# The scan's output kept channel-major: the state as the stationary operand, the decay as a loaded tile, the skip term through DRAM

## The chip, the cores and the metric

The kernel runs on one core of a Trainium2 chip. The metric is device time in microseconds (us) of one execution; lower is better. One further execution was recorded by the hardware profiler, and all rows shown here come from it.

## What is computed

Two layers of a diffusion backbone run over 128 context tokens and 512 latent tokens: layer 0 is gated attention, layer 1 a bidirectional state-space scan (Mamba-2 SSD). The change is in layer 1's scan. Cut to what matters:

```python
def ssd_chunked(x, a, b, c, h0):           # chunks of 128 tokens, 4 groups of 8 heads of 64 channels
    a_cs = jnp.cumsum(a, axis=2)
    decay = jnp.exp(jnp.where(lower, a_cs[:, :, :, None] - a_cs[:, :, None, :], -jnp.inf))
    cb = jnp.einsum('bclgn,bcsgn->bclsg', c, b)
    y_diag = jnp.einsum('bclsgr,bcsgrp->bclgrp', cb[..., None] * decay, x)
    states = jnp.einsum('bclgn,bclgrp->bcgrpn', b, x * decay_end[..., None])
    ...                                     # h_prev: the state ahead of each chunk
    y_off = jnp.einsum('bclgn,bcgrpn->bclgrp', c, h_prev) * jnp.exp(a_cs)[..., None]
    return (y_diag + y_off).reshape(Bs, T, H, P), h_final
...
    y = y_f + flip(y_b) + d_skip.astype(f32)[:, None] * xs
    y = rms_norm(y.reshape(B, T, D_INNER) * jax.nn.silu(z), gnorm_w)
    return y @ w_out, h_f, h_b
```

## The kernel before

The 640 tokens are five tiles `t` of 128 (t=0 is the context, t=1 to 4 the latents). Layer 1 (`layer1`, L1010) first projects; then four groups `g` of 8 heads run one after the other, and within a group a loop over ten steps `j` (L1240) lays out the scan, in the midst of which the projections for the next group (`x_unit`, `bc_unit`) and for the gate (`z_unit`) are placed. A projection is 48 matmuls (L914) into one of two PSUM buffers `pj`; `conv_chunk` then takes it through three DVE steps, a tanh on ACT and a last DVE step (L994 to L999) into a tile `u` (two buffers) or `B0`/`B1`. `x_turn` transposes `u` on PE so that tokens lie on partitions, and ACT copies that into `xt`. Weights come in through SP's DMA queue and are split in two parts by ACT (L73) and by DVE or POOL (L74).

The scan of a group, in the program's order:

- `y_init` (L1107): POOL writes the skip term, `xt` times the head's skip weight, into Y, tokens on partitions.
- `a_load`, `decay`: the logarithms of the decay come by DMA from DRAM (`acd`), broadcast over partitions, into tiles `am0` (two buffers) and `am1` (one buffer); POOL masks them (L1116, L1117), ACT takes 16 exponentials (L1121), POOL adds the two directions (L1122). `mix` multiplies by C times B (PE L1127, DVE L1128).
- `off` (L1173 to L1175), twice per step for the two directions: PE multiplies C (stationary) with the state `H` (512 columns); DVE multiplies the result in PSUM by exp of the cumulated decay, a column `ea` broadcast over each head's 64 channels, and adds it to Y.
- `diag` (L1135 to L1140): 16 half-width matmul instructions give the chunk's own part with channels on partitions; four transposes on PE (L1138) turn Y round; ACT copies the diagonal part into Y (L1139), and DVE adds the turned Y (L1140). From here on Y is channel-major.
- `advance` (L1179 to L1183) moves the state on; `weighted` (POOL) and `prompt_state` (L1151) belong to the states.
- `gate` multiplies Y by the gate and stores it to DRAM (`yzd`, L1091); in group 3 `gate_last` does so tile by tile, and the output projection (L1368) begins within the group.

The order of the instructions on each engine is laid out by the framework's scheduler, which goes by a model of the engines and by which instruction is ready; each engine, and SP's DMA queue, then works in that order. Two PSUM pools exist: `pj` (two buffers of two banks) and `a` (four of one bank), the latter for all small results.

Of the kernel before, what the change touches and what calls it, by code (L numbers as in the profile page):

```python
# [10 lines left out]
AF = mybir.ActivationFunctionType  # L11
ALU = mybir.AluOpType
# [4 lines left out]
P = 128  # L17
D = 1024
KD = D // P
NT = 5  # L20
# [5 lines left out]
SH = 32  # L26
NG = 4
# [8 lines left out]
def uoff(t):  # L36
    return col0(t) - 1
# [16 lines left out]
class Hybrid:  # L54
# [862 lines left out]
    def dt_stage(self, hT, wp, pj, pa, sp, wk):  # L917
        nc, A = self.nc, self.A
        w = self.load_w(wp, A["l1_w_in"], [(DI + DI + 2 * NG * P, 64)])
        W = NT * 64  # L920
# [3 lines left out]
        ones, al, db = misc[:, 0:P], misc[:, P:P + 64], misc[0:64, 199:200]  # L924
        packs = [self.tl(wk, [P, 3, NT, 64], tag=t_, bufs=b_) for t_, b_ in (("am0", 2), ("am0", 2), ("am1", 1))]
        slots = iter([p_[:, i] for p_ in packs for i in range(3)])
        self.dsk = self.tl(sp, [P, SH], tag="dsk")
        for d, s in enumerate(("f", "b")):
            nc.sync.dma_start(out=db[32 * d:32 * d + 32, :], in_=A[f"l1_dt_bias_{s}"].unsqueeze(1))
            nc.sync.dma_start(out=al[:, 32 * d:32 * d + 32], in_=A[f"l1_a_log_{s}"].unsqueeze(0).to_broadcast([P, 32]))  # L930
        nc.sync.dma_start(out=self.dsk, in_=A["l1_d_skip"].unsqueeze(0).to_broadcast([P, SH]))
        nc.scalar.activation(al, al, AF.Exp)
        ps = self.proj_T(pj, w, 0, 64, hT)
        dtv = self.tl(wk, [64, TW], tag="Wl", bufs=1)
# [6 lines left out]
        T = lambda nme, pool=None: next(slots) if pool is None else self.tl(pool, shp, tag=nme)  # L941
        v, u, s, s2, p_, dt = T("sv"), T("su"), T("ss_"), T("ss2"), T("spp"), T("sdt")
# [21 lines left out]
        acs = T("sacs")  # L964
# [1 line left out]
        nc.vector.memset(ones, 1.0)  # L966
        ptot = self.tl(pa, shp, tag="a")
        nc.tensor.matmul(ptot, ones, a_, start=True, stop=True)
        self.ea, self.cd, self.ws, self.nb = T("ea", sp), T("cd", sp), T("ws", sp), T("nb", sp)
        nc.scalar.activation(self.ea, acs, AF.Exp)  # L970
        nc.scalar.activation(self.cd, ptot, AF.Exp)
        nc.vector.tensor_tensor(self.ws, ptot, acs, op=ALU.subtract)
        nc.scalar.activation(self.ws, self.ws, AF.Exp)
# [3 lines left out]
        pr = self.tl(pj, [P, 1024], tag="pj")  # L977
        for t in range(NT):
            nc.tensor.transpose(pr[0:64, P * t:P * t + P], acs[:, t, :], self.ident)
        at = self.tl(wk, [64, NT * P], tag="Wh", bufs=1)  # L980
        nc.scalar.copy(at, pr[0:64, 0:NT * P])
        self.acd = [[self.tl(self.dp, [2, 8, P], tag=f"acd{t}{g}") for g in range(NG)] for t in range(NT)]
        for g in range(NG):
            for d in range(2):
                for t in range(NT):
                    r0 = 32 * d + 8 * g
                    nc.sync.dma_start(out=self.acd[t][g][d], in_=at[r0:r0 + 8, P * t:P * t + P])

    def conv_chunk(self, j, w, off, hT, pj, u):
        nc = self.nc  # L990
# [19 lines left out]
    def layer1(self, hT, wp, pj, pa, ctx):  # L1010
        nc, tc, A, O = self.nc, self.tc, self.A, self.O
        sp = self.pool("s1", ctx=ctx)
        self.weng = [nc.gpsimd]
        wk = self.pool("s2", bufs=2, ctx=ctx)
        self.fss = self.tl(self.cp, [P, NT], tag="fss")
        self.one = self.tl(self.cp, [P, 1], tag="one")
        nc.vector.memset(self.one, 1.0)
        self.ssq = self.tl(sp, [P, NT, P], tag="ssq")
        self.yzd = [self.tl(self.dp, [P, NT, 4, P], tag=f"yzd{g}") for g in range(NG - 1)]
        Y = self.Y = self.tl(sp, [P, NT, 4, P], tag="ys")  # L1020
        bcs, xts, zss, W, Xw, H, St = {}, {}, {}, {}, {}, {}, {}
        wcur = {}

        def x_unit(g, jj):
# [4 lines left out]
            wcur["u"] = self.conv_chunk(4 * g + jj, wcur["x"], P * (jj % 2), hT, pj, self.tl(wk, [P, TW - 3], tag="u"))  # L1029

        def x_turn(g, jj):
            xt = xts[g]
            self.turn(wcur["u"], pa, lambda t, ps: nc.scalar.copy(xt[:, t, P * jj:P * jj + P], ps))

        def bc_unit(g, which):
            if which == 0:
# [63 lines left out]
        bch = lambda ap: ap.unsqueeze(2).to_broadcast([P, 8, HD])  # L1100
        h3 = lambda ap: ap.rearrange("p (h d) -> p h d", d=HD)
        sl = lambda g, d: slice(32 * d + 8 * g, 32 * d + 8 * g + 8)
        ts = lambda t: slice(uoff(t), uoff(t) + P)

        def y_init(g, t):
            y = Y[:, t].rearrange("p j q -> p (j q)")
            nc.gpsimd.tensor_tensor(h3(y), h3(xts[g][:, t, :]), bch(self.dsk[:, 8 * g:8 * g + 8]), op=ALU.mult)  # L1107

        def a_load(g, t):
            af = W[g, t] = [self.tl(wk, [P, 8, P], tag=f"am{d}", bufs=2 - d) for d in range(2)]  # L1110
            for d in range(2):
                nc.sync.dma_start(out=af[d].rearrange("p h l -> p (h l)"), in_=self.acd[t][g][d].rearrange("h l -> (h l)").unsqueeze(0).to_broadcast([P, 8 * P]))
# [17 lines left out]
        def diag(g, t):  # L1130
            w = W.pop((g, t))[0]
            pd = self.tl(pa, [P, 4, P], tag="a")
            for h in range(8):
                e = 64 * (h % 2)
                nc.tensor.matmul(pd[e:e + 64, h // 2, :], xts[g][:, t, HD * h:HD * h + HD], w[:, h, :], start=True, stop=True)  # L1135
            pr = self.tl(pa, [P, 4, P], tag="a")
            for i in range(4):
                nc.tensor.transpose(pr[:, i, :], Y[:, t, i, :], self.ident)  # L1138
            nc.scalar.copy(Y[:, t], pd)  # L1139
            nc.vector.tensor_tensor(Y[:, t], Y[:, t], pr, op=ALU.add)  # L1140

        def weighted(g, t, d):
            xw = Xw[g, t, d] = self.tl(wk, [P, 512], tag=f"xw{d}", bufs=2)
# [24 lines left out]
            nc.scalar.copy(H[d], ps.rearrange("p j q -> p (j q)"))  # L1168

        def off(g, t, d):  # L1170
            y = Y[:, t].rearrange("p j q -> p (j q)")
            ps = self.tl(pa, [P, 512], tag="a")
            nc.tensor.matmul(ps, bcs[g][1][:, ts(t)], H[d], start=True, stop=True)  # L1173
            nc.vector.tensor_tensor(h3(ps), h3(ps), bch(self.ea[:, t, sl(g, d)]), op=ALU.mult)
            nc.vector.tensor_tensor(y, y, ps, op=ALU.add)  # L1175

        def advance(g, t, d):
            p2 = self.tl(pa, [P, 512], tag="a")
# [49 lines left out]
        for g in range(NG):  # L1228
# [11 lines left out]
            for j in range(10):  # L1240
# [19 lines left out]
                    diag(g, t)  # L1260
                if j < 4:
                    a_load(g, seq[j + 1])
                if j <= 2:
                    for d in range(2):
                        weighted(g, j + 1 if d == 0 else 4 - j, d)
# [199 lines left out]
```

## Time and profile before

| | |
|---|---|
| time, three runs | 996.47 us median (991.88 to 997.28) |
| profiled execution | 996.55 us, of which 994.8 us are the span from the first to the last instruction |
| busy share of the span | PE 94%, DVE 66%, ACT 52%, POOL 43% |
| mean granted clock of PE | 0.981 of full speed |
| DMA | 127.91 MB, on average 129 GB/s |

PE is TensorE's matmul, PEld its weight loads, DVE VectorE, ACT ScalarE, POOL GpSimd, SP SyncE (which only issues DMAs here). Busy shares are averages over stages with different limits. "a <- b" in a list of waits reads: a waited, and b ended the wait; an engine's name with a "q" is its sequencer. L12 is line 12 of the kernel.

### The profile page before, as it was taken

The page shows a single profiled execution, that of the slowest core. Times are in us where ns is not written, and L with a number is a line of the kernel's source. Part 1 is how long each engine was busy: PE and PEld are TensorE (multiplying, and loading weights), DVE is VectorE, ACT ScalarE, POOL GpSimd, SP SyncE. Part 2 cuts the span into 40 slices and gives each one's busy share as a digit, 9 for nine tenths or more (in the row PEclk, how much of TensorE's full clock was granted, in tenths as well). Part 3 has the DMA queues.
Part 4 walks back from the last instruction along what each step waited for, and adds up shares of the span by engine and source line. Part 5 has one row for each costly group of instructions (what it writes and reads, how often), then busy time and mean ns, then how long its engine had stood idle before and what let it go on. Part 6 is the DMA issues. An engine that isn't in the chain of part 4 may idle for free. (4 is left out here: it accounts for less than half of the span.)

```text
span 994.8 us, 17000 instructions
## 1 busy us (share of the span) xinstructions
PE 937.9 (94%) x6466; PEld 835.0 (84%) x6466; DVE 656.3 (66%) x1046; ACT 515.3 (52%) x1212; POOL 431.1 (43%) x415
## 2 busy tenths in 40 slices
PE   5998999999999989989899979999999999989998
PEld 3897879879997789989898878889988898658786
DVE  5468665666675764884759854956587547797663
ACT  5355666757775763433446564446436642554240
POOL 3345235227270162364267475739484853333000
PEclk9999999999999989999999999999999999989999
DMA  9942234221113222333234352344524441455752
GB/s 319 351 128 87 86 127 138 67 73 43 37 49 107 85 93 100 123 106 89 86 131 148 121 181 88 109 139 145 151 87 146 156 133 64 128 183 190 257 194 96
DMA packets 90354, 127.91 MB, mean 129 GB/s; under 512 B 6816, under 2 KB 65312, under 8 KB 90272
## 3 DMA queue, kind: packets, MB, share of 16 engines
q1 hardware_dynamic: 90272, 126.82, 39.6%
q8 instruction: 51, 0.84, 0.3%
q14 instruction: 31, 0.25, 0.1%
HBM read 115.10 MB, written 11.70 MB: 127 GB/s over the span
## 5 line engine op out<-in xcount | busy, mean ns | idle before, releaser
L914 PE MATMUL pj<-h,wh 128*128 128x322 f32 (+1 forms) x1248 | 298.3, 325 | 8.7 <-DVE B L999 7.5
L914 PEld LDWEIGHTS pj<-h,wh 128*128 128x128 f32 (+1 forms) x1248 | 211.2, 189 | 21.5 <-issue 14.0
L74 POOL TENSOR_TENSOR wl<-raw,wh 128x512 fp32r<-128x512 f32 (+1 forms) x70 | 133.1, 1912 | 184.6 <-ACT wh L73 182.9
L914 PE MATMUL pj<-h,wl 128*128 128x322 f32 (+1 forms) x624 | 198.6, 319 | 0.0
L73 ACT CAST wh<-raw 128x1024 fp32r<-128x1024 f32 (+1 forms) x117 | 103.0, 912 | 79.7 <-DMA raw<-in_l_w_out 22.4
L1121 ACT ACTIVATE am<-am,nb 128x128 f32<-128x128 f32 x320 | 97.9, 389 | 62.4 <-POOL am L1117 39.9
L914 PEld LDWEIGHTS pj<-h,wl 128*128 128x128 f32 (+1 forms) x624 | 118.2, 190 | 3.9 <-issue 3.6
L283 PE MATMUL pp<-wh,big 128*128 128x256 f32 x576 | 112.1, 284 | 0.5 <-ACT sg L527 0.5
L283 PEld LDWEIGHTS pp<-wh,big 128*128 128x128 f32 x576 | 91.2, 188 | 0.9 <-ACT sg L527 0.7
L74 DVE TENSOR_TENSOR wl<-raw,wh 128x1024 fp32r<-128x1024 f32 x47 | 62.8, 1347 | 38.0 <-ACT wh L73 38.0
L283 PE MATMUL pp<-wl,big 128*128 128x256 f32 x288 | 81.1, 282 | 0.0
L74 DVE TENSOR_TENSOR pl<-pt,ph 128x512 fp32r<-128x512 f32 (+1 forms) x100 | 59.2, 599 | 25.9 <-ACT ph L73 25.1
L633 DVE TENSOR_REDUCE nm<-S 128x1 f32<-128x640 f32 x64 | 52.3, 819 | 13.7 <-PE S L630 12.7
L73 ACT CAST ph<-pt 128x512 fp32r<-128x512 f32 (+1 forms) x100 | 51.4, 517 | 19.1 <-PE pt L658 14.3
L1122 POOL TENSOR_TENSOR am<-am,am 128x1024 f32<-128x1024 f32 x20 | 48.7, 2437 | 26.2 <-ACT am L1121 26.2
L637 ACT ACTIVATE Pt<-S,nm 128x640 f32<-128x640 f32 x64 | 51.2, 802 | 13.4 <-PE pt L658 9.9
L1368 PE MATMUL pj<-wh,h 128*128 128x512 f32 x160 | 54.4, 413 | 0.5 <-ACT wh L73 0.5
L283 PEld LDWEIGHTS pp<-wl,big 128*128 128x128 f32 x288 | 54.3, 188 | 0.0
L658 PE MATMUL pt<-cst,Pt 128*128 128x128 f32 x320 | 51.6, 279 | 2.6 <-DVE pl L74 2.3
L630 PE MATMUL S<-kT,qT 128*128 128x320 f32 x256 | 51.1, 324 | 2.3 <-ACT Pt L637 2.3
L1116 POOL TENSOR_SCALAR_AFFINE_SELECT am<-am 128x1024 f32<-128x1024 f32 x20 | 24.2, 1211 | 56.6 <-DMA am<-acd 32.3
L658 PEld LDWEIGHTS pt<-cst,Pt 128*128 128x128 f32 x320 | 37.2, 142 | 11.8 <-PE S L630 3.7
(347 smaller groups left out, 2135.9 us busy)
## 6 DMA issues: line engine op xcount, KB each, us to landing
raw<-in_l_w_in SPq DMA_DIRECT2D x48, 512.0 KB
am<-acd SPq DMA_DIRECT2D x40, 512.0 KB
raw<-in_l_w_out SPq DMA_DIRECT2D x36, 512.0 KB
og<-in_l_mod_w SPq DMA_DIRECT2D x29, 512.0 KB
raw<-in_l_w_in SPq DMA_DIRECT2D x25, 256.0 KB
mw<-in_l_mod_w SPq DMA_DIRECT2D x11, 512.0 KB
raw<-in_l_mod_w SPq DMA_DIRECT2D x8, 512.0 KB
yzd<-ys SPq DMA_DIRECT2D x6, 640.0 KB
```

The lines of the kernel that those rows point to most:

```text
L73: (heng.tensor_copy if heng else self.nc.scalar.copy)(hi, src)
L74: (eng or self.nc.vector).tensor_tensor(lo, src, r32(hi), op=ALU.subtract)
L283: nc.tensor.matmul(ps, a[:, k, cs], b[:, k, :], start=k == 0 and a is hi and b is w[0], stop=k == KD - 1 and a is lo)
L630: nc.tensor.matmul(S[:, 192 + 320 * q:512 + 320 * q], qTs[g, t][:, h, :], kT[:, hl, 320 * q:320 * q + 320], start=hl == 0, stop=hl == 1)
L633: nc.vector.tensor_reduce(c["m"], c["s"], axis=AX.X, op=ALU.max, negate=True)
L637: nc.scalar.activation(Pt, c["s"], AF.Exp, bias=c["m"], scale=1.0, accum_out=rss[g][t][:, h:h + 1])
L658: nc.tensor.transpose(pt[:, 2 * i + j, :], Pts[j][:, kt * P:kt * P + P], self.ident)
L914: nc.tensor.matmul(ps[0:m, 190 + 322 * half:512 + 322 * half], w[b][:, k, off:off + m], hT[s][:, k, 322 * half:322 * half + 322], start=fi ...
L1116: nc.gpsimd.affine_select(out=af[0], in_=af[0], pattern=[[0, 8], [1, P]], base=0, channel_multiplier=-1, compare_op=ALU.is_ge, fill=NEG)
L1121: nc.scalar.activation(af[d][:, h, :], af[d][:, h, :], AF.Exp, bias=self.nb[:, t, i:i + 1], scale=1.0)
L1122: nc.gpsimd.tensor_tensor(af[0], af[0], af[1], op=ALU.add)
L1368: nc.tensor.matmul(self.PS[t][n], y[a][:, kk, :], b, start=k0 + k == 0 and i == 0, stop=k0 + k == 15 and i == 2)
```

## The change

Y stays channel-major from the start. In `off` the state becomes the stationary operand (four matmuls of 128 columns) and C the moving one. The factor exp(cumulated decay) now varies along the free axis and differs by partition half, so it is computed once for all (`et`), stored to DRAM (`ecd`) and loaded, broadcast over 64 partitions twice, into a tile E (four buffers) by a new function `e_load`. The skip term is made by ACT from `u`, in place and after `u` has been transposed, stored to DRAM (`dud`), and loaded into Y by `y_init`. `diag` adds its PSUM result to Y with one DVE operation; the four transposes and ACT's copy go, and with them the tile `ea`.

```diff
-        self.dsk = self.tl(sp, [P, SH], tag="dsk")
+        self.dsk = self.tl(sp, [P, SH // 2], tag="dsk")
...
-        nc.sync.dma_start(out=self.dsk, in_=A["l1_d_skip"].unsqueeze(0).to_broadcast([P, SH]))
+        dv = A["l1_d_skip"].rearrange("(c a) -> a c", a=2)
+        for a in range(2):
+            nc.sync.dma_start(out=self.dsk[64 * a:64 * a + 64, :], in_=dv[a].unsqueeze(0).to_broadcast([64, SH // 2]))
...
-        nc.scalar.activation(self.ea, acs, AF.Exp)
...
+        et = self.tl(wk, [64, NT * P], tag="Wl", bufs=1)
+        nc.scalar.activation(et, at, AF.Exp)
+        self.ecd = self.tl(self.dp, [64, NT * P], tag="ecd")
+        nc.sync.dma_start(out=self.ecd, in_=et)
...
         def x_turn(g, jj):
-            xt = xts[g]
-            self.turn(wcur["u"], pa, lambda t, ps: nc.scalar.copy(xt[:, t, P * jj:P * jj + P], ps))
+            xt, u = xts[g], wcur["u"]
+            self.turn(u, pa, lambda t, ps: nc.scalar.copy(xt[:, t, P * jj:P * jj + P], ps))
+            nc.scalar.activation(u, u, AF.Copy, scale=self.dsk[:, 4 * g + jj:4 * g + jj + 1])
+            nc.sync.dma_start(out=self.dud[g][:, 1:5, jj, :], in_=u[:, 0:4 * P].rearrange("p (t q) -> p t q", q=P))
+            nc.sync.dma_start(out=self.dud[g][:, 0, jj, :], in_=u[:, uoff(0):uoff(0) + P])
...
         def y_init(g, t):
-            y = Y[:, t].rearrange("p j q -> p (j q)")
-            nc.gpsimd.tensor_tensor(h3(y), h3(xts[g][:, t, :]), bch(self.dsk[:, 8 * g:8 * g + 8]), op=ALU.mult)
+            nc.sync.dma_start(out=Y[:, t], in_=self.dud[g][:, t])
...
-            pr = self.tl(pa, [P, 4, P], tag="a")
-            for i in range(4):
-                nc.tensor.transpose(pr[:, i, :], Y[:, t, i, :], self.ident)
-            nc.scalar.copy(Y[:, t], pd)
-            nc.vector.tensor_tensor(Y[:, t], Y[:, t], pr, op=ALU.add)
+            nc.vector.tensor_tensor(Y[:, t], Y[:, t], pd, op=ALU.add)
+
+        def e_load(g, t, d):
+            e = E[d] = self.tl(wk, [P, 4, P], tag="E", bufs=4)
+            r = 32 * d + 8 * g
+            for a in range(2):
+                src = self.ecd[r:r + 8, P * t:P * t + P].rearrange("(j a) l -> a j l", a=2)[a]
+                nc.sync.dma_start(out=e[64 * a:64 * a + 64], in_=src.unsqueeze(0).to_broadcast([64, 4, P]))
...
         def off(g, t, d):
-            y = Y[:, t].rearrange("p j q -> p (j q)")
-            ps = self.tl(pa, [P, 512], tag="a")
-            nc.tensor.matmul(ps, bcs[g][1][:, ts(t)], H[d], start=True, stop=True)
-            nc.vector.tensor_tensor(h3(ps), h3(ps), bch(self.ea[:, t, sl(g, d)]), op=ALU.mult)
-            nc.vector.tensor_tensor(y, y, ps, op=ALU.add)
+            ps = self.tl(pa, [P, 4, P], tag="a")
+            for j in range(4):
+                nc.tensor.matmul(ps[:, j, :], H[d][:, P * j:P * j + P], bcs[g][1][:, ts(t)], start=True, stop=True)
+            nc.vector.tensor_tensor(ps, ps, E[d], op=ALU.mult)
+            nc.vector.tensor_tensor(Y[:, t], Y[:, t], ps, op=ALU.add)
...
                 if j < 4:
                     a_load(g, seq[j + 1])
+                    for d in range(2):
+                        e_load(g, j + 1 if d == 0 else 4 - j, d)
```

## Rows read from the trace of the kernel before

**Rows 1.** The page: busy time, share of the span, instructions.

```profile
PE 937.9 (94%) x6466; PEld 835.0 (84%) x6466; DVE 656.3 (66%) x1046; ACT 515.3 (52%) x1212; POOL 431.1 (43%) x415
```

**Rows 2.** Busy time by stretch: length, engines (instructions), PE clock, DMA share, GB/s.

```profile
500.00:850.00 350.00, 337.89 (x2248) 304.86 (x2247) 229.30 (x272) 178.62 (x447) 214.60 (x149) 1.00 0.41 129
850.00:915.00 65.00, 58.06 (x286) 43.92 (x285) 55.63 (x69) 35.90 (x69) 21.47 (x26) 0.92 0.54 173
915.00:995.00 80.00, 74.92 (x323) 60.02 (x321) 45.03 (x57) 21.79 (x25) 1.59 (x1) 1.00 0.52 179
```

**Rows 3.** What PE waited for from 500 to 850 us: total, times, longest.

```profile
PE pj L914 <- DVE B L999: 7.5, 2, 5.2
PE a L1138 <- DVE ys L1175: 1.8, 3, 1.0
```

**Rows 4.** The same list of waits, 850 to 915 us.

```profile
PE a L1135 <- DVE ys L1175: 2.3, 1, 2.3
PE a L1138 <- DVE ys L1175: 1.8, 1, 1.8
```

**Rows 5.** L1138 alone by stretch: PE and PEld busy (instructions), clock, DMA.

```profile
500.00:850.00 350.00, 10.33 (x64) 6.95 (x64) 1.00 0.41 129
850.00:915.00 65.00, 2.54 (x16) 1.75 (x16) 0.92 0.54 173
```

**Rows 6.** Chain of waits: start us, us, what, how many.

```profile
802.83 7.18 PE pj L914 x48
810.01 0.87 PE a L1166 x8
```

**Rows 7.** Timeline of PE: start us, us, line, operation, tiles, shapes, how many.

```profile
569.03 1.02 PE L1173 MATMUL a<-h,B 128*128 128x512 f32 x2
569.88 1.05 PE L1151 MATMUL a<-T,xw 128*128 128x128 f32 x8
```

**Rows 8.** Line L1151, its weight loads: ns least/median/most, first and last start.

```profile
L1151 PEld LDWEIGHTS a<-T,xw x64: 186/192/192, 569.5 to 896.1; 128*128 128x128 f32 x64
```

**Rows 9.** Groups, 440 to 850 us: busy us, mean ns | idle before, releasers.

```profile
L1175 DVE TENSOR_TENSOR ys<-ys,a 128x512 f32<-128x512 f32 x28 | 18.9, 680 | 4.8 <-POOL ys L1107 4.3
...
L1107 POOL TENSOR_TENSOR ys<-xt,dsk 128x512 f32<-128x512 f32 x20 | 21.1, 1088 | 12.9 <-DMA yzd<-ys 4.6 <-ACT xt L1033 4.4 <-DVE xt L1058 2.1
...
L998 ACT ACTIVATE pj<-u 128x641 f32<-128x641 f32 x16 | 11.2, 701 | 33.1 <-DVE u L996 33.1
...
L1140 DVE TENSOR_TENSOR ys<-ys,a 128x512 f32<-128x512 f32 x16 | 10.9, 683 | 18.2 <-ACT ys L1139 18.1
...
L1139 ACT COPY ys<-a 128x512 f32<-128x512 f32 x16 | 9.3, 579 | 27.5 <-PE a L1138 18.8 <-issue 8.8
```

**Rows 10.** Loads of the state, their issue on SP: ns least/median/most.

```profile
L1160 SPq DMA_DIRECT2D st<-in_state_bwd_l x4: 453/478/516, 446.6 to 701.9; - x4
```

**Rows 11.** The page: the DMA queue's packets, MB, share of 16 engines.

```profile
q1 hardware_dynamic: 90272, 126.82, 39.6%
```

**Rows 12.** Chain of waits, near the end: two landings, a store's and a load's.

```profile
925.68 3.96 DMA out_y_sample<-ym
...
937.50 2.64 DMA u<-yzd
```

**Rows 13.** Timeline of ACT, SP and DVE around the reuse of a buffer `u`.

```profile
644.81 0.24 ACT L1033 COPY xt<-a 128x128 f32<-128x128 f32 x1
...
637.51 15.62 SPq L1112 DMA_DIRECT2D am<-acd  x3
...
655.00 0.95 DVE L994 TENSOR_SCALAR u<-pj,cw,cols 128x641 f32<-128x641 f32 x1 [0.34 <-PE pj L914]
```

**Rows 14.** Timeline of ACT and DVE in group 0; brackets: idle time, releaser.

```profile
574.68 2.45 ACT L1121 ACTIVATE am<-am,nb 128x128 f32<-128x128 f32 x8 [3.12 <-POOL am L1117]
...
577.63 0.69 DVE L1140 TENSOR_TENSOR ys<-ys,a 128x512 f32<-128x512 f32 x1 [4.63 <-ACT ys L1139]
...
579.71 1.22 DVE L1128 TENSOR_TENSOR am<-am,a 128x1024 f32<-128x1024 f32 x1 [1.39 <-POOL am L1122]
```

More of the change, by code (lines that the diff above doesn't have):

```diff
@@ L968, in dt_stage @@
         nc.tensor.matmul(ptot, ones, a_, start=True, stop=True)
-        self.ea, self.cd, self.ws, self.nb = T("ea", sp), T("cd", sp), T("ws", sp), T("nb", sp)
-        nc.scalar.activation(self.ea, acs, AF.Exp)
+        self.cd, self.ws, self.nb = T("cd", sp), T("ws", sp), T("nb", sp)
         nc.scalar.activation(self.cd, ptot, AF.Exp)
@@ L1018, in layer1 @@
         self.ssq = self.tl(sp, [P, NT, P], tag="ssq")
+        self.dud = [self.tl(self.dp, [P, NT, 4, P], tag=f"dud{g}") for g in range(NG)]
         self.yzd = [self.tl(self.dp, [P, NT, 4, P], tag=f"yzd{g}") for g in range(NG - 1)]
         Y = self.Y = self.tl(sp, [P, NT, 4, P], tag="ys")
-        bcs, xts, zss, W, Xw, H, St = {}, {}, {}, {}, {}, {}, {}
+        bcs, xts, zss, W, Xw, H, St, E = {}, {}, {}, {}, {}, {}, {}, {}
         wcur = {}
```

## The prediction

> **What bounds the kernel now.** I read the page first: TensorE (PE) is busy 94% of the span [rows 1]. That is an average, so next I read the busy time by stretch, cut where layer 1's scan begins and ends [rows 2]. From 500 to 850 us PE works 337.89 of 350 us at full clock (1.00), VectorE (DVE) only 229.30, ScalarE (ACT) 178.62 and GpSimd (POOL) 214.60: in this stretch, which holds groups 0 to 2 of the scan and the start of group 3, PE sets the pace. From 850 to 915 us PE has 58.06 of 65 and DVE 55.63, and the clock is 0.92: group 3's end runs at the pace of DVE and of what feeds it. After 915 us only output projections are left. Then I asked what PE waits for. In the scan it is mostly DVE's last step of a conv (7.5 us in two waits), then the transposes of Y, which wait for DVE's additions to Y (1.8 us in three waits) [rows 3]. In the end stretch the waits for Y are 2.3 and 1.8 us [rows 4]. So a microsecond of PE work taken out between 500 and 850 us should be nearly a microsecond of span, as long as the next PE instruction is ready; one taken out behind 850 us need not be.
>
> **Transposes of Y removed (L1137 to L1138).** 80 of them, 64 between 500 and 850 us and 16 behind [rows 5]. Their busy time of 10.33 us overlaps with neighbours, so I price them by pace: eight transposes of the same shape take 0.87 us on the chain, 0.109 us each, and a projection step is 7.18 us for 48, 0.150 us each [rows 6]. 64 x 0.109 = 7.0 us on the path. The other 16, 1.7 us, lie where DVE sets the pace; I count them at nothing. The waits of these transposes for Y go with them: 1.8 us in the scan [rows 3] and 1.8 us behind it [rows 4]; both count, 3.6 us. The 2.3 us of `diag`'s own matmul behind `ys L1175` [rows 4] is a wait for a PSUM buffer, which may or may not stay; not counted.
>
> **`off` turned round (L1173).** One matmul of 512 columns becomes four of 128 with four different stationary tiles. Each fp32 call shows as two instructions: the old pair starts at 569.03 us and the next form follows at 569.88, so 0.43 us each, 0.85 us a call. The four matmuls of `prompt_state`, also 128x128 against 128 columns with a new stationary tile each, are the new form exactly: eight instructions in 1.05 us, of which the last one's own 0.275 us is tail, so 0.111 us each, 0.89 us a call [rows 7]. So +0.04 us on 32 calls, 1.2 us in all. From the row that it equals I take +1.2; the bounds are 0 and the case in which the weight loads show (rival 4). The rule that speaks against the change is the Trainium skill's, "TensorE: Matmul & The Clock Gate", section "LDWEIGHTS (loading the stationary operand)": a weight load takes time by its columns alone, 128 / 1.2 = 107 ns here, so four times the stationary tiles mean four times the load time; by that figure six more loads on 32 calls would be an estimated 20 us if none overlapped. Here a load is recorded with 192 ns [rows 8] and still the eight of them come at 0.111 us: in this trace they overlap with the matmuls before them.
>
> **Work of the other engines.** `diag` loses its ACT copy (20 x 0.58 us) and keeps one DVE addition of the same size (0.68 us), now straight from PSUM; `off` keeps two DVE operations, the first with a loaded tile in place of the broadcast column, which I price like its neighbour, 0.68 us [rows 9]. DVE: no change. ACT gains one scaling of `u` in each of 16 `x_turn` calls, by the nearest row (the tanh over 641 columns) 0.70 us, and an exponential over 640 columns in place of one over 320: +11.2 + 0.3 - 11.6 = about 0. POOL loses 20 `y_init` at 1.09 us, 22 us [rows 9]; it is not the bound, so nothing is counted, and what it frees (the chain of the decay tiles on POOL and ACT) belongs to rival 1.
>
> **DMAs.** Added on SP's queue: 64 for E (128 KB each), 32 stores of the scaled `u`, 20 loads of Y, 1 for `ecd`, and one more for the skip vector: 118. An issue costs SP about 0.48 us [rows 10], so 57 us of SP time over some 375 us; SP is an in-order queue that mostly waits. Bytes: 8.4 + 5.2 + 5.2 + 0.2 = 19 MB; at 39.6% of the engines for 126.82 MB [rows 11] that is 5.9% of the span, or 17% more of the 350 us on top of 0.41 [rows 2]; with packets of 512 B perhaps somewhat more. The DMA engines have room, so I count no slowing.
> E: its tile has four buffers, a buffer's last reader is the `off` of two steps earlier, and a step of the loop is a projection of 48 x 0.150 = 7.2 us plus scan work. A load needs its two issues and a landing of 2.6 to 4.0 us [rows 12]; hidden. If the cover is gone, DVE's first product of `off` waits, and with it all that is queued on DVE: the conv steps and the weight split.
> Y at the head of a group: SP waits for the store of the group before, as POOL did; then t=1, the first one wanted, is there after two issues and a landing, 2 x 0.48 + 2.64 to 3.96 = 3.6 to 4.9 us, where POOL needed 2 x 1.09 = 2.2. At three group heads that is +4.2 to +8.1 us if DVE's wait reaches PE, 0 if PE has a projection in hand, and, if the Y waits behind POOL end altogether, a gain of 4.3 us (DVE idle before `ys L1175` [rows 9]). I take 0, as PE shows no wait ended by POOL here [rows 3].
> `u`: a buffer of two. Until now PE's five transposes freed it; now the scaling on ACT, two issues on SP and the landing of a store do. A place where SP is also taken is in group 1: ACT has copied the transposes by 645.05 us, the scaling would end near 645.8, and DVE writes into that buffer at 655.00 us [rows 13]. Without a queue the store is down at 645.8 + 1.0 + 4.0 = 650.8: hidden by 4.2 us. With a queue it may not be (rival 3).
>
> **The sum.** The profiled execution takes 996.55 us (span 994.8 and 1.75 around it; the median of the three runs is 996.47, so the two can be used alike). 996.55 - 7.0 - 3.6 + 1.2 = 987.2. In group 0, though, PE's next long wait, 5.2 us behind a conv of B [rows 3], is set by DVE behind a chain that runs through DMA, POOL and ACT: ACT's exponentials wait for POOL, DVE's `ys L1140` for ACT, DVE's `am L1128` for POOL until 579.71 us [rows 14]. PE's savings of that group, 20 x 0.109 = 2.2 us less 0.3 for its `off`s, become more of that wait. So **989.1 us**, with 985 to 993 as its own range (the Y loads at the group heads, the 1.7 us of the last group, the 2.3 us of PSUM wait).
>
> **Rivals.**
> 1. *The waits go too.* DVE sits 18.2 us idle before `ys L1140`, for ACT's copy [rows 9], and ACT's queue is blocked by it. The change takes that hop out, so conv steps and exponentials move up, and PE's waits for a conv (7.5 us) [rows 3] and for PSUM (2.3 us) [rows 4] shrink. All gone: 989.1 - 7.5 - 2.3 = 979. Against it: DVE's next instruction in [rows 14] waits for POOL anyway.
> 2. *PE's savings turn into waits in other groups as well.* A second wait for a conv of B lies in group 2 (7.5 - 5.2 = 2.3 us) [rows 3]. If the chain of decay tiles or DVE sets the pace there too, another 1.9 us is lost, and the waits for Y behind 850 us are taken over by DVE's weight split (1.8), and one Y load shows (1.4): 989.1 + 5.1 = 994.
> 3. *Slower: the stores of the scaled `u` are stuck on SP.* SP issues in order, and from 637.51 us it sits 15.62 us on three loads of decay tiles, each waiting for its buffer, until 653.13 [rows 13]. A store queued behind them lands 4.5 to 5 us later, near 658, and DVE, which wants the buffer at 655.00, stands some 3 us with its whole queue. A buffer is reused like this at eight places (two in the x projections of each of the four groups); 8 x 3 = 24 us, less what PE's second projection buffer covers; I take 20: 1009. It decides when a store reaches SP more than about 4 us behind a blocked load. Against it: raw weight loads and stores pass between such waits, so the order of the queue follows what is ready.
> 4. *The weight loads of the new `off` do not overlap.* 6 more at 0.19 us [rows 8] on 32 calls are 36 us: 1025. The pace in [rows 7] speaks against it. By the figure of the Trainium skill that is named under `off` ("TensorE: Matmul & The Clock Gate", "LDWEIGHTS (loading the stationary operand)") this case would give an estimated 1009.
>
> **How the numbers follow.** Forecast 0.45, rival 1 0.17, rival 2 0.18, rival 3 0.17, rival 4 0.03. A measurement tells about 0.5% from no change, so faster means below 991.5 us and slower above 1001.5. Faster: 0.40 of the forecast and all of rival 1, 0.57, and 0.01 of rival 2, 0.58. Same: the rest of the forecast and rival 2, 0.22, and the mild end of rival 3, 0.02, so 0.24. Slower: 0.18. The range runs from rival 1's far end to the mild end of rival 3, 978 to 1002; outside lie rival 4 and most of rival 3.
>
> **What would show it.** Right: no transposes of Y; a call of `off` at about 0.89 us; PE busy in the scan down by some 6 us with its waits about as long; ACT's waits for PE before the copy gone; no DVE wait for E. Rival 3 shows as DVE idle before `u L994` ended by a DMA of `dud`; the Y loads as DVE idle before `ys` ended by a DMA; rival 4 as `off` at 1.2 us or more a call. The prediction is wrong if waits of PE that the trace of before does not have add up to more than some 5 us: the order of each queue is laid out anew for the changed program, and no row tells what it will be.

## The result and the profile after

The changed kernel takes 1006.33 us (median of 5 runs, 1003.78 to 1013.16) against 996.47 for the kernel before in the same job (5 runs, 991.88 to 997.42): a ratio of 1.0107, 95% interval 1.0065 to 1.0148. It is slower by about 10 us where 989.1 was forecast, and lies outside the range of 978 to 1002. The profiled execution is the longest of the five, 1013.16 us with a span of 1011.4, so the rows below name places and sizes of single waits; what a part is worth in all is taken from medians.

The page first: busy time of the engines, the packets, and SP's DMA queue.

```profile
PE 933.7 (92%) x6578; PEld 846.2 (84%) x6578; DVE 661.5 (65%) x1046; ACT 516.7 (51%) x1208; POOL 412.6 (41%) x395
DMA packets 123413, 146.98 MB, mean 145 GB/s; under 512 B 10624, under 2 KB 95744, under 8 KB 123328
q1 hardware_dynamic: 123328, 145.85, 46.5%
```

PE has 4.2 us less work than in [rows 1], and the 19 MB are what the forecast counted against [rows 11]; the span is 16.6 us longer all the same. So PE waits more. Its waits by stretch begin to show it ahead of the scan, where the forecast had nothing. This is the list of PE's waits from 425 to 460 us (total, times, longest), first of the kernel before, then of the changed one:

```profile
PE pj L242 <- DVE xn L877: 2.6, 2, 1.9
```

```profile
PE pj L242 <- DVE xn L877: 14.7, 2, 12.9
```

One wait of 12.9 us in place of one of under 2. What leads to it stands on SP's queue and on ACT (timeline of the changed kernel: start us, length us, engine, line, operation; a run of issues on SP includes the time between them; brackets: idle time and releaser):

```profile
429.27 0.32 SPq L872 DMA_DIRECT2D x1d<-y  x1
429.64 1.52 SPq L933 DMA_DIRECT2D dsk<-in_l_d_skip  x2
434.74 0.40 SPq L83 DMA_DIRECT2D raw<-in_l_w_in  x1
439.67 4.41 SPq L872 DMA_DIRECT2D x1d<-y  x1
444.18 10.78 SPq L83 DMA_DIRECT2D raw<-in_l_w_in  x2
...
452.58 0.62 ACT L73 CAST wh<-raw 128x512 fp32r<-128x512 f32 x1 [12.33 <-DMA raw<-in_l_w_in]
```

The two loads of the skip vector (L933) are issued at 429.64. The weight load issued at 434.74 lands only at 452.58, 17.8 us later, and ACT stands 12.33 us for it; the store of `x1d`, issued in 0.32 us ahead of L933, takes SP 4.41 us behind it. Behind ACT stands DVE, and behind DVE's `xn` PE. What the DMA engines do meanwhile (busy time by stretch, as in [rows 2]; the last three columns are PE's clock, the DMA share and GB/s):

```profile
432.00:447.00 15.00, 9.45 (x64) 8.68 (x63) 8.02 (x9) 2.24 (x6) 7.84 (x6) 1.00 0.05 0
450.00:456.00 6.00, 0.00 (x0) 0.00 (x0) 2.25 (x3) 1.66 (x3) 2.22 (x2) 0.50 0.64 202
456.00:460.00 4.00, 3.47 (x14) 2.92 (x15) 1.74 (x3) 0.46 (x1) 1.53 (x2) 0.50 0.62 189
464.00:470.00 6.00, 6.00 (x43) 6.00 (x42) 0.49 (x1) 0.44 (x1) 0.00 (x0) 1.00 0.00 0
500.00:850.00 350.00, 328.64 (x2312) 311.10 (x2310) 227.56 (x261) 183.59 (x445) 188.53 (x124) 0.99 0.61 177
```

From 432 to 447 us the share is 0.05 and 0 GB/s move. The trace's packets of that stretch are all of 4 bytes, 102 to 116 of them in each microsecond; in all the two loads are 2048 packets, one for each element. Only when they have run out does data flow again (202 GB/s from 450 us). PE's clock falls in this wait: PE does nothing from 450 to 456 us, the granted clock is 0.50 (1.2 GHz) up to 460, where 14 matmuls keep it busy for 3.47 us, and 1.00 (2.4 GHz) again from 464 us, where 43 take 6.00.

The scan is the second place. From 500 to 850 us PE works 328.64 us where [rows 2] has 337.89, and its waits there (500 to 870 us), which answer [rows 3], are many and small, ended by several engines; the whole list adds up to 21.3 us, where the kernel before has 14.1. (The changed kernel's scan begins later, so the same window does not hold quite the same work.)

```profile
PE pj L914 <- DVE B L1004: 6.7, 3, 2.9
PE a L1143 <- ACT wh L73: 3.2, 1, 3.2
PE a L1190 <- ACT xt L1039: 2.2, 1, 2.2
PE a L1143 <- DVE h L1194: 2.0, 1, 2.0
PE pj L914 <- DVE zs L1067: 1.9, 1, 1.9
PE a L1162 <- DVE ys L1144: 1.8, 1, 1.8
```

SP, which issues the new transfers of the skip term, now stands in order for the scaling of `u` (L1040) ahead of its store (L1041), and for the store of the last group's Y ahead of the loads of the next (L1115); 460 to 930 us:

```profile
SPq L1041 <- ACT u L1040: 45.2, 10, 10.5
SPq L1115 <- DMA yzd<-ys: 11.0, 3, 4.7
```

What became of the parts that the forecast priced, first the new `off` on PE (timeline; it answers [rows 7]), then groups of operations from 460 to 930 us as in [rows 9] (busy, mean ns | idle before, releaser):

```profile
551.31 1.95 PE L1184 MATMUL a<-B,h 128*128 128x128 f32 x16
```

```profile
L1185 DVE TENSOR_TENSOR a<-a,E 128x512 f32<-128x512 f32 x32 | 21.8, 691 | 3.2 <-PE a L1184 3.2
L1186 DVE TENSOR_TENSOR ys<-ys,a 128x512 f32<-128x512 f32 x32 | 21.6, 679 | 6.2 <-DMA ys<-dud 6.1
L1040 ACT ACTIVATE u<-u,dsk 128x641 f32<-128x641 f32 x16 | 13.4, 839 | 0.0
L1144 DVE TENSOR_TENSOR ys<-ys,a 128x512 f32<-128x512 f32 x20 | 13.4, 680 | 3.5 <-PE a L1143 3.5
```

Sixteen matmul instructions of two calls take 1.95 us. Without the last one's tail of 0.275 that is 1.675 us for the 15 steps from one start to the next, 0.112 us each: the pace that was forecast. DVE never waits for E. It waits for Y 6.1 us at three group heads, where it waited 4.3 us for POOL before ([rows 9]).

### The profile page after: what moved, and what is told of

Read it like the earlier page. It is cut to its first block, busy times and chain, and to the rows that moved or that the text cites. A ratio compares the mean times of both kernels' runs of the same rounds, so it can differ in the third digit from the quotient of the medians.

```text
span 1011.4 us, 17424 instructions
## 1 busy us (share of the span) xinstructions
PE 933.7 (92%) x6578; PEld 846.2 (84%) x6578; DVE 661.5 (65%) x1046; ACT 516.7 (51%) x1208; POOL 412.6 (41%) x395
## 5 line engine op out<-in xcount | busy, mean ns | idle before, releaser
L914 PE MATMUL pj<-h,wh 128*128 128x322 f32 (+1 forms) x1248 | 293.8, 323 | 10.5 <-DVE B L1004 6.7
L914 PEld LDWEIGHTS pj<-h,wh 128*128 128x128 f32 (+1 forms) x1248 | 213.6, 192 | 20.2 <-issue 14.6
L914 PE MATMUL pj<-h,wl 128*128 128x322 f32 (+1 forms) x624 | 201.5, 323 | 0.0
L74 DVE TENSOR_TENSOR wl<-raw,wh 128x1024 fp32r<-128x1024 f32 x47 | 66.4, 1417 | 39.0 <-ACT wh L73 38.9
L1381 PE MATMUL pj<-wh,h 128*128 128x512 f32 x160 | 52.2, 400 | 0.0
L841 PE MATMUL a<-wh,big 128*128 128x256 f32 x256 | 46.8, 283 | 0.0
```

The costliest lines, as they stand in the source:

```text
L74: (eng or self.nc.vector).tensor_tensor(lo, src, r32(hi), op=ALU.subtract)
L841: self.nc.tensor.matmul(ps, self.ohl[a][:, k, ts], w[b][:, k, :], start=k == 0 and i == 0, stop=k == KD - 1 and i == 2)
L914: nc.tensor.matmul(ps[0:m, 190 + 322 * half:512 + 322 * half], w[b][:, k, off:off + m], hT[s][:, k, 322 * half:322 * half + 322], start=fi ...
L1381: nc.tensor.matmul(self.PS[t][n], y[a][:, kk, :], b, start=k0 + k == 0 and i == 0, stop=k0 + k == 15 and i == 2)
```

## Experiments

The theory from here on has two parts. **A:** the two loads of the skip vector, element by element, block the DMA engines and cost about 10 us ahead of the scan. **B:** the skip term's way through SP and DRAM costs about as much again in the scan, while the part that the forecast was about (no transposes, `off` turned) gains what it was to gain. The rivals are that the early wait is covered elsewhere and the whole loss lies in the scan, that `off` or E costs what is lost, and that the gain never came. Ratios are to the kernel before, run on the same chip beside each.

**1. The skip vector in whole rows.** Of the changed kernel:

```diff
-        dv = A["l1_d_skip"].rearrange("(c a) -> a c", a=2)
+        dw = self.tl(sp, [P, SH // 2, 2], tag="dskw")
+        nc.sync.dma_start(out=dw.rearrange("p c a -> p (c a)"), in_=A["l1_d_skip"].unsqueeze(0).to_broadcast([P, SH]))
         for a in range(2):
-            nc.sync.dma_start(out=self.dsk[64 * a:64 * a + 64, :], in_=dv[a].unsqueeze(0).to_broadcast([64, SH // 2]))
+            nc.vector.tensor_copy(self.dsk[64 * a:64 * a + 64, :], dw[64 * a:64 * a + 64, :, a])
```

> The changed kernel with one difference: the skip weights come in as one broadcast load of whole rows (128 B a partition), as before, and two small DVE copies pick the even or the odd heads for each half. Theory 1 (the two new loads of the skip weights, element by element, 4 B a packet, keep SP's queue busy from 431 to about 450 us of the trace of after, the weight load behind them is late, and PE waits 12.9 us instead of 0.8): this wait goes back to about 1 us, time 1006.3 - 12 = about 994. Rival (the loss is made in the scan, by SP standing at the stores of the scaled u, and the early wait is an accident of the profiled execution): the time stays within 2 us of 1006.

Measured: 995.05 us, ratio 0.9986 (0.9966 to 1.0006). One load of 128-byte rows and two DVE copies in place of 8 KB in 4-byte packets give back 11.3 us of 1006.33 (by the two ratios, each to the kernel before beside it, about 12). PE's waits from 425 to 460 us, and the stretch that had 0 GB/s:

```profile
PE pj L242 <- DVE xn L877: 4.8, 2, 2.9
```

```profile
432.00:447.00 15.00, 9.77 (x66) 8.79 (x64) 12.11 (x14) 3.14 (x8) 9.73 (x7) 1.00 0.42 122
```

The longest wait is 2.9 us instead of 12.9: 10.0 us less in one row of the two profiles, near the whole difference. What is left, no gain against the kernel before, is the scan's.

**2. The same two loads added to the kernel before**, into a tile that nobody reads:

```diff
+        dx = self.tl(sp, [P, SH // 2], tag="dskx")
+        dv = A["l1_d_skip"].rearrange("(c a) -> a c", a=2)
+        for a in range(2):
+            nc.sync.dma_start(out=dx[64 * a:64 * a + 64, :], in_=dv[a].unsqueeze(0).to_broadcast([64, SH // 2]))
```

> The kernel before, unchanged but for two more loads at the same place: the skip weights element by element into a tile that nobody reads. Theory 1: the loads alone cost what they cost in the changed kernel, PE waits about 12 us more near 445 us, time 996.5 + 12 = about 1008. Rival (the wait belongs to the new order of the instructions, not to these loads): within 2 us of 996.5.

Measured: 1002.34 us, ratio 1.0058 (1.0038 to 1.0078), so +5.8 of 996.5 and less than in the changed kernel. The order on SP differs (the second load is issued at 435.10 us, behind a weight load instead of ahead of it), and PE's longest wait is 5.4 us:

```profile
PE pj L242 <- DVE xn L877: 7.3, 2, 5.4
```

So the loads cost time by themselves, about half of the 12 us that were expected. That the difference comes from which weight load lies behind them is read from the order on SP; it was not varied alone.

**3. The stores of `u` issued by ACT** (on top of 1):

```diff
-            nc.sync.dma_start(out=self.dud[g][:, 1:5, jj, :], ...)
-            nc.sync.dma_start(out=self.dud[g][:, 0, jj, :], ...)
+            nc.scalar.dma_start(out=self.dud[g][:, 1:5, jj, :], ...)
+            nc.scalar.dma_start(out=self.dud[g][:, 0, jj, :], ...)
```

> As e1_dsk_whole, and the two stores of the scaled u in each x_turn are issued from ACT's own DMA queue in place of SP's. Theory 2 (what is left of the loss comes from SP standing 45 us in all at these stores, waiting for ACT's scaling, with loads of decay tiles and weights behind them; POOL's waits for decay tiles rose from 65 to 110 us): SP no longer stands there, POOL's waits for decay tiles fall below 80 us, and the time is 3 to 6 us below e1_dsk_whole, about 989. Rival (these waits have cover; the added DMA traffic or the new order sets the end): within 2 us of e1_dsk_whole.

Measured: 991.63 us, ratio 0.9961 (0.9944 to 0.9977), 3.4 us better than 1. The waits of POOL for the decay tiles' loads, which were expected to shrink, did not (102.9 us in all, 98.2 in run 1), so the gain does not come by that way.

**4. The skip term left out** (on top of 1: no scaling, no stores; POOL clears Y in place of the loads):

```diff
-            nc.scalar.activation(u, u, AF.Copy, scale=self.dsk[:, 4 * g + jj:4 * g + jj + 1])
-            nc.sync.dma_start(out=self.dud[g][:, 1:5, jj, :], ...)
-            nc.sync.dma_start(out=self.dud[g][:, 0, jj, :], ...)
...
-            nc.sync.dma_start(out=Y[:, t], in_=self.dud[g][:, t])
+            nc.gpsimd.memset(Y[:, t], 0.0)
```

> As e1_dsk_whole, with the skip term left out of the computation: no scaling of u on ACT, no stores, no loads of Y; POOL sets Y to zero at the head of a group instead. This bounds what the whole path of the skip term costs. Theory 2: the path costs 5 us or more, so about 988. Rival (the path is hidden and the loads of E or the order set the end): within 2 us of e1_dsk_whole, about 994.

Measured: 985.18 us, ratio 0.9894 (0.9864 to 0.9924), 9.9 us better than 1. What the change is built round is a gain of 11 us; the skip path takes 10 of it and the skip vector 11 more.

**5. The skip term in place.** On top of 1, the conv writes into the next group's Y, ACT scales it there after the transposes, and stores and loads go. Y has two buffers, E three in place of four, and the tile `u` is gone.

```diff
+                Ys[g] = self.tl(sp, [P, 4, TW - 3], tag="ys", bufs=2)
...
-            wcur["u"] = self.conv_chunk(..., self.tl(wk, [P, TW - 3], tag="u"))
+            wcur["u"] = self.conv_chunk(..., Ys[g][:, jj, :])
...
-            nc.sync.dma_start(out=self.dud[g][:, 1:5, jj, :], ...)
-            nc.sync.dma_start(out=self.dud[g][:, 0, jj, :], ...)
...
-            nc.sync.dma_start(out=Y[:, t], in_=self.dud[g][:, t])
```

> The changed kernel with the skip vector in whole rows and the skip term without DRAM: the conv writes into the next group's Y itself, ACT scales it there after the transposes, and the stores of u and the loads of Y are gone (Y has two buffers, E three instead of four). Theory (the way of the skip term through SP and DRAM costs the 10 us between 995 and 985): 985 to 988. Rival (ACT's 16 scalings of 0.83 us stand in front of the copies and exponentials and are the cost): 992 to 995. Rival (what is left is the cost of the E loads): no better than the run with the skip term left out, 985, and worse with one buffer of E less: 988 to 990.

Measured: 983.43 us, ratio 0.9859 (0.9822 to 0.9897): the whole computation, faster than both kernels, and 11.6 us better than 1. ACT's 16 scalings are still there, so they are not the cost. The second buffer of Y is new here, but run 4 has one buffer and comes within 2 us. PE's waits from 500 to 870 us:

```profile
PE a L1142 <- issue: 6.6, 5, 2.5
PE a L1013 <- DVE ys L1005: 2.8, 3, 1.4
PE pj L914 <- DVE zs L1067: 1.9, 2, 1.3
PE a L1189 <- DVE am L1135: 0.6, 1, 0.6
PE pj L914 <- DVE B L1005: 0.4, 1, 0.4
```

No wait of 3 us is left, and of the 6.7 us for a conv of B in the changed kernel 0.4 remain.

**6. No loads of Y, scalings and stores kept** (on top of 1; POOL clears Y as in 4):

```diff
-            nc.sync.dma_start(out=Y[:, t], in_=self.dud[g][:, t])
+            nc.gpsimd.memset(Y[:, t], 0.0)
```

> The changed kernel with the skip vector in whole rows, and the 20 loads of Y replaced by a clearing of Y on POOL; the scalings and the stores stay, so the skip term is missing in the output. Theory (SP standing at the stores of u for ACT is the larger share of the skip path's 10 us): 990 to 993. Rival (the Y loads at the head of a group are the larger share): 986 to 988.

Measured: 991.69 us, ratio 0.9958 (0.9938 to 0.9978), 3.4 us better than 1: the time of the theory. Its reason, SP's stand for ACT, is tested in run 8.

**7. The element-wise loads issued by POOL** (of the changed kernel):

```diff
-            nc.sync.dma_start(out=self.dsk[64 * a:64 * a + 64, :], ...)
+            nc.gpsimd.dma_start(out=self.dsk[64 * a:64 * a + 64, :], ...)
```

> The changed kernel with its two element-wise loads of the skip vector issued by POOL instead of SP, nothing else. Theory (the 2048 packets of 4 bytes hold up what is queued behind them on the same queue only): 995 to 998, PE's wait near 443 us back at 3 us or less. Rival (they hold up all of the core's DMA engines, whichever queue they come from): 1003 to 1007, PE's wait near 443 us again 10 us or more.

Measured: 1003.64 us, ratio 1.0078 (1.0046 to 1.0111): the time of the rival, though not its place. The wait near 443 us is gone, for POOL issues the loads later; another comes in its stead. The stretch by windows, SP's timeline and PE's waits from 425 to 475 us:

```profile
432.00:447.00 15.00, 10.55 (x72) 9.57 (x71) 12.52 (x13) 3.36 (x9) 12.31 (x10) 1.00 0.69 18
```

```profile
439.55 4.87 SPq L83 DMA_DIRECT2D raw<-in_l_w_in  x2
444.51 5.94 SPq L922 DMA_DIRECT2D xs<-in_cst  x1
450.50 4.86 SPq L929 DMA_DIRECT2D xs<-in_l_dt_bias_f  x1
```

```profile
PE pj L914 <- ACT wh L73: 6.5, 1, 6.5
PE pj L242 <- DVE xn L877: 3.7, 2, 1.9
```

SP issues nothing element-wise here, and yet the single issues at L922 and L929 take it 5.94 and 4.86 us (0.46 and 0.42 us in run 1), and its weight load comes late. So the packets hold up what other queues issue too. The Trainium skill says as much of queues in "DMA: Bandwidth & Descriptors", "Rules for kernel authors": DMAs spread over SP, ACT and GpSimd run on the same 16 engines and interleave. This run agrees: of the 11.3 us only 2.7 were got back by the medians, and the intervals of the two ratios overlap.

**8. No scaling of `u`**, stores and loads kept (on top of 1), so the skip term is added unscaled:

```diff
-            nc.scalar.activation(u, u, AF.Copy, scale=self.dsk[:, 4 * g + jj:4 * g + jj + 1])
```

> The changed kernel with the skip vector in whole rows and ACT's 16 scalings of u left out, so that the skip term is added unscaled; stores and loads stay where they are. Theory (SP stands at the stores until ACT has scaled; without the scaling the stores follow the conv): 990 to 992, and SP's waits for ACT at the stores of 34 us gone. Rival (the number of issues and the traffic of 17 us a group is the cost, not the wait): 994 to 996.

Measured: 997.53 us, ratio 1.0011 (0.9990 to 1.0033), no better than 1. SP's stand for ACT at the stores, 45.5 us in run 1, is gone (21.8 us for DVE's conv stand there now), and nothing is won. So the wait for ACT's scaling is not the cost; that SP stands there at all is not ruled out by this run.

**9. Stores on ACT, loads of Y on POOL** (on top of 3):

```diff
-            nc.sync.dma_start(out=Y[:, t], in_=self.dud[g][:, t])
+            nc.gpsimd.dma_start(out=Y[:, t], in_=self.dud[g][:, t])
```

> The changed kernel with the skip vector in whole rows, the stores of the scaled u issued by ACT and the loads of Y issued by POOL: the skip term still goes through DRAM with the same bytes, but SP issues none of it. Theory (what the skip path costs is SP, which stands in order at its stores and loads with weight loads and decay tiles behind it): 986 to 988, both savings of 3.4 us found so far adding up. Rival (the traffic itself, a DMA share of 0.61 against 0.53 without it, delays the weight loads, or a wait on ACT or POOL takes SP's place): 991 or more, like the run with the stores alone on ACT.

Measured: 998.24 us, ratio 1.0015 (0.9994 to 1.0036): 6.6 us worse than 3, so the two savings do not add up. With SP free of all the skip term's issues the loss is there in full; it is not SP's order alone. DVE's waits for the loaded Y are the longest of all versions:

```profile
DVE ys L1187 <- DMA ys<-dud: 8.6, 3, 4.2
```

**10. E loaded once in a group** (on top of 5; 16 loads in place of 64):

```diff
         def e_load(g, t, d):
+            if t not in (1, 4) or (t == 1) != (d == 0):
+                return
```

> The version with the skip term in place (983.4), with each direction's E tile loaded once in a group and used for all four steps, 16 loads in place of 64, so that the decay of three steps in four is wrong in the output. Theory (the E loads are hidden, as the forecast had it): 982 to 985. Rival (SP's 48 issues, its 52.6 us of waits for a buffer of E and 6.3 MB of traffic cost time): 976 to 980.

Measured: 983.30 us, ratio 0.9870 (0.9839 to 0.9900), the same as 5. The E loads are hidden, as forecast.

**11. The kernel before without its transposes of Y**, nothing else changed:

```diff
-            pr = self.tl(pa, [P, 4, P], tag="a")
-            for i in range(4):
-                nc.tensor.transpose(pr[:, i, :], Y[:, t, i, :], self.ident)
-            nc.scalar.copy(Y[:, t], pd)
-            nc.vector.tensor_tensor(Y[:, t], Y[:, t], pr, op=ALU.add)
+            nc.vector.tensor_tensor(Y[:, t], Y[:, t], pd, op=ALU.add)
```

> The kernel before with nothing but the 80 transposes of Y and ACT's copy left out, DVE adding the diagonal block straight from PSUM, so that the output mixes two layouts. Theory (the forecast's terms for the transposes and their waits, 7.0 and 3.6 us, less 1.9 given back in group 0): 987 to 990. Rival (the waits for a conv shrink too, as DVE and ACT run ahead): 979 to 984. Rival (the waits only change their place): 993 to 996.

Measured: 983.42 us, ratio 0.9881 (0.9841 to 0.9921): 11.9 us by the ratio, between 7.9 and 15.9. The median lies in the first rival's range; the interval reaches into the theory's. PE's row of the page, and its waits for a conv of B from 500 to 870 us:

```profile
PE 926.7 (95%) x6386; PEld 825.8 (84%) x6386; DVE 664.0 (68%) x1046; ACT 506.4 (52%) x1192; POOL 432.4 (44%) x415
```

```profile
PE pj L914 <- DVE B L999: 3.6, 4, 2.1
```

PE has 11.2 us less work than in [rows 1], and the waits for a conv of B halve (7.5 us with a longest of 5.2 in [rows 3]).

**12. Stores on ACT and no loads of Y** (3 and 6 together):

```diff
-            nc.sync.dma_start(out=self.dud[g][:, 1:5, jj, :], ...)
-            nc.sync.dma_start(out=self.dud[g][:, 0, jj, :], ...)
+            nc.scalar.dma_start(out=self.dud[g][:, 1:5, jj, :], ...)
+            nc.scalar.dma_start(out=self.dud[g][:, 0, jj, :], ...)
...
-            nc.sync.dma_start(out=Y[:, t], in_=self.dud[g][:, t])
+            nc.gpsimd.memset(Y[:, t], 0.0)
```

> The changed kernel with the skip vector in whole rows, the stores of the scaled u issued by ACT, and no loads of Y (POOL clears Y), so that the skip term is missing in the output. Theory (off SP the stores cost next to nothing; the loads are the rest of the skip path's cost): 984 to 987. Rival (the stores' traffic or ACT's scalings cost by themselves, the loads little): 989 to 992.

Measured: 987.80 us, ratio 0.9916 (0.9894 to 0.9938), between the two expectations: scaling and stores, off SP, cost 2.6 us against 4.

**13. Loads of Y alone** (on top of 1; all from group 0's store, and no scaling or store in the other groups):

```diff
-            nc.sync.dma_start(out=Y[:, t], in_=self.dud[g][:, t])
+            nc.sync.dma_start(out=Y[:, t], in_=self.dud[0][:, t])
...
+            if g:
+                return
             nc.scalar.activation(u, u, AF.Copy, scale=self.dsk[:, 4 * g + jj:4 * g + jj + 1])
```

> The changed kernel with the skip vector in whole rows, scalings and stores for group 0 alone, and all 20 loads of Y from group 0's store, so that the skip term is wrong in groups 1 to 3. Theory (SP's waits at the stores and the loads cost about 3.4 us each and something more together): 990 to 993. Rival (the loads alone carry nearly all): 994 to 997. Rival (the loads cost nothing once no store of u stands ahead of them on SP): 985 to 988.

Measured: 1000.58 us, ratio 1.0048 (1.0028 to 1.0068), above all that was expected: 15.4 us over run 4, and 5.5 over run 1, which has all the stores and scalings besides. The waits of POOL for the decay tiles, 460 to 880 us, of this run and then of run 12:

```profile
POOL am L1127 <- DMA am<-acd: 56.4, 10, 11.9
POOL am L1128 <- DMA am<-acd: 46.7, 15, 6.4
```

```profile
POOL am L1126 <- DMA am<-acd: 52.7, 15, 5.9
POOL am L1125 <- DMA am<-acd: 28.9, 9, 8.5
```

103.1 us with the loads, 81.6 without. But run 9 has 78.9 us there and takes 998.2, so this wait does not settle it.

**What the runs tell of the skip path.** The five versions with the 20 loads of Y and a whole-row skip vector lie at 991.6 to 1000.6 us (runs 3, 1, 8, 9, 13), the five without the loads at 983.3 to 991.7 (10, 5, 4, 12, 6). That the path through DRAM costs 10 to 12 us is shown (1 against 4 and 5). Where it is lost, and where the skip vector's 11 us are, the first and the last matmul of `off` tell (the lines of `off` on PE: duration in ns, then first and last start; the kernel before, the changed one, run 1, run 5):

```profile
L1173 PE MATMUL a<-h,B x64: 590/592/697, 522.1 to 871.9; 128*128 128x512 f32 x64
L1184 PE MATMUL a<-B,h x256: 270/275/377, 536.0 to 885.2; 128*128 128x128 f32 x128
L1185 PE MATMUL a<-B,h x256: 270/275/377, 525.1 to 871.2; 128*128 128x128 f32 x128
L1183 PE MATMUL a<-B,h x256: 271/275/275, 522.9 to 857.9; 128*128 128x128 f32 x128
```

The scan begins 10.9 us earlier in run 1 than in the changed kernel: that is the skip vector. From first to last it takes 346.1 us in run 1 and 335.0 in run 5: that is the path through DRAM. It reaches PE as many small waits: the whole list from 500 to 870 us adds up to 14.4 to 19.8 us in the five versions with the loads and to 10.4 to 15.4 in the five without.

Which part of the path is the larger is open. Leaving out the loads wins 3.4 and 3.8 us (6 against 1, 12 against 3), leaving out the scalings and stores too wins another 6.5 and 2.6 (4 against 6 and 12), and yet the loads nearly alone (13) cost 15.4. Which wait carries it is open as well: taking SP's wait for ACT away won nothing (8), moving the loads off SP lost 6.6 us (9 against 3), and DVE's own wait for Y is 5 to 9 us in all of them against 4.3 for POOL before. The order of the queues is laid out anew for each version, and run 13 against run 1 shows that this alone can be worth 5 us; no version was tried in which the loads change and the order is held.

## Why the prediction was wrong

**The steps add up.** From 996.5 us: without the transposes 983.4 (run 11); with `off` turned, E loaded and the skip term in place 983.4 (5); with the skip term through DRAM 995.05 (1); with the skip vector element by element 1006.3. Each is a median of its own job, and runs 11 and 5 differ in several things at once, so that turning `off` and loading E come to nothing is a net result. The forecast had the direction of the first two steps right and their size wrong: it took them for a gain of 7.4 us, and run 5 has about 13 (between 10.3 and 17.7), below the forecast's own range of 985 to 993 and near rival 1. For the last two, 11.6 and 11.3 us, it held nothing.

**The step that failed first** is in the part on DMAs: "1 for `ecd`, and one more for the skip vector: 118", each an issue of 0.48 us, and "The DMA engines have room, so I count no slowing". By bytes and issues the loads are nothing, 8 KB in two issues of 1.52 us together. But their source is a vector read with a step of two, so every element is a packet of its own: 2048 packets at some 106 a microsecond are 19 us in which next to nothing else moves. The estimate asked how many bytes and issues, and not how many packets. The forecast listed only the scan and never looked at what is queued on SP ahead of it, where `dt_stage` loads its constants and layer 1's first weight loads pass. The Trainium skill has the rule, in "DMA: Bandwidth & Descriptors", "Rules for kernel authors": a strided last dimension becomes one descriptor for each element, and the last dimension should be made contiguous. The trace agrees: 2048 packets of 4 bytes for 2048 elements. Run 1 gives the price here.

**The second** is "Y at the head of a group", with bounds of -4.3 to +8.1 us, of which 0 was taken, together with "hidden by 4.2 us" for the stores. Stores, loads and scalings cost 10 to 12 us in all. DVE's wait for Y, 6.1 us, lies inside the bounds given, but only 1.8 more than before; the rest is spread over waits which no term of the sum held. The sentence that the order of each queue is laid out anew and no row tells what it will be stood under what would make the prediction wrong, with "more than some 5 us" of new waits as the mark. It is what happened: PE's waits from 440 to 940 us add up to 23.1 us before, 42.5 in the changed kernel and 30.6 in run 1. By itself this second step would have left the time inside the range (run 1, 995.05 us), though 6 us above the forecast; the skip vector took it out.

**Transposes and their waits.** Forecast 7.0 + 3.6, less 1.9 given back in group 0: 8.7 us. Run 11: 11.9, with an interval that holds 8.7. PE lost 11.2 us of work, near the 12.87 of [rows 5], where the pace of 0.109 us gives 8.7 for all 80. Where the other 2.5 come from is open (the mean clocks of the two profiles, 0.981 and 0.983, differ a little too), and so is whether the 16 behind 850 us count. The give-back in group 0 did not come: the longest wait for a conv of B fell from 5.2 to 2.1 us instead of growing. That is the mechanism of rival 1, "the waits go too", and it goes against the reading of [rows 14] that DVE would wait for POOL anyway.

**`off` turned round.** 0.112 us a matmul where 0.111 was forecast; rival 4 did not occur, and of the 20 us estimated beside this term nothing is seen, as [rows 7] had it. **DVE, ACT and E** came out near their prices: 691 ns for the product with E where 680 was taken, and 839 ns in place of 701 for the scaling (2.2 us over 16), which run 5 shows to cost nothing. E is hidden (run 10).

**Rival 3**, the only slower one besides rival 4, has the result's sign and nearly its time (1009), and the wrong mechanism. In it a store of `u` is stuck behind a blocked load, and DVE stands for the buffer of `u`. What the trace shows is the reverse: the store itself blocks SP, 45.2 us in ten waits for ACT, and DVE never waits for a store of `u`. And run 8, with the stand at the stores cut to 21.8 us, is no faster. **Rival 2** (994) is near run 1, the change without the skip vector, but by another cause.

## What to carry over

Price a DMA by its packets, not by its bytes or issues: look at the innermost step of the access pattern on both sides, and at which loads stand behind it at the place where it is issued, even when the transfer itself is needed much later. A term that can be made in place in SBUF should not go through DRAM because "the DMA engines have room": a share of 0.41 was no proof that 10 MB more would be free. And split a many-part change by its parts before judging it: here the idea was worth 13 us, and two side details took 23.

## What the hardware showed

From 432 to 447 us the 4-byte packets pass at 102 to 116 per microsecond over the 16 engines, which gives an estimated 0.15 us of an engine for each, although the trace records them with 7 to 9 ns; so the DMA share reads 0.05 while the engines take nothing else of account. Issued by POOL the same loads are recorded as 32 packets of 256 bytes at some 8.2 us each, 0.13 us for each of a packet's 64 elements, and the share reads 0.69 (run 7). In both cases single issues of SP behind them take 4 to 6 us, where run 1 has 0.3 to 0.5. A share of busy DMA time, like a busy engine, therefore tells little where packets are tiny; the rate in GB/s (0 and 18) tells more.
